# Zero-filled head tiles for the score products of two attentions, and other PSUM banks for half of the gating products

## The chip, the core and the metric

One Trainium2 chip; the kernel runs on one of its cores. The metric is device time in microseconds (us) of one execution, the median of several runs. TensorE (PE in the profile) does the matrix products, VectorE (DVE), ScalarE (ACT) and GpSimd (POOL) the rest, SyncE (SP) issues most transfers.

## The reference, cut to what matters

Two blocks over 512 tokens of 1024 features. The three places that the change touches:

```python
def chunk_band_attention(q, k, v, rel_bias):          # block 1, 8 heads of 64
    ...
    scores = jnp.einsum('bnqhd,bnkhd->bnhqk', qc, kb).astype(jnp.float32) * (d ** -0.5)
    ...
    scores = jnp.where(valid[None, :, None, None, :], scores + bias[None, None], NEG_INF)
    p = jax.nn.softmax(scores, axis=-1)
    out = jnp.einsum('bnhqk,bnkhd->bnqhd', p.astype(vb.dtype), vb)

# block 1, behind attention (y_a) and a linear recurrence (y_b)
merged = gate_a * (y_a @ proj_a[l]) + gate_b * (y_b @ proj_b[l])

def forgetting_attention(q, k, v, f_pre):             # block 2, layer 0, 8 heads of 64
    ...
    logits = jnp.einsum('bhqd,bhkd->bhqk', qb, k).astype(jnp.float32) * scale + fq[..., :, None] - F[..., None, :]
    logits = jnp.where(kpos[None, :] <= qpos[:, None], logits, -jnp.inf)
    p = jax.nn.softmax(logits, axis=-1)
```

## The kernel before, in words

**Dense products.** Activations lie with features on partitions and are split into a high and a low part; so are the weights, chunk by chunk: a DMA brings `raw`, ACT makes `whi` (L132), DVE makes `wlo` (L133). `dense_A` (L163) multiplies 256 output features at a time into two PSUM banks of [128, 512] with three products (high by high, low by high, high by low). The two banks come from a pool `mm` of two banks, unless the caller hands banks in (`ps=`). `dense_B` (L281) does the same with tokens on partitions.

**Attention** (`attention1` in block 1, the second half of `layer0` in block 2) runs in two halves of four heads. A half projects q, k and v for its heads. Two heads share a [128, 512] tile of q and one of k: the even head has rows 0 to 63, the odd one rows 64 to 127. Each of the two PSUM banks of a projection is evacuated in one ACT instruction over 128 rows (L1538 in block 1, L846 in block 2), with the factor 0.125, and in block 2 a bias, put on q.

`attention_heads` then goes over 16 units a half (4 heads by 4 query tiles of 128), software-pipelined: scores of unit u, transposes of unit u-1, values of unit u-2. A score (L1569) multiplies the 64 rows of its head, 128 queries against 128, 256, 384 or 512 keys; in f32 each is issued as two matmuls. In block 2 a bf16 matmul over 128 rows adds the causal mask (L1571). DVE adds the bias and finds the row minimum of the negated scores (L1573, `sb`, `sm`), ACT takes the exponential (L1575), PE transposes (L1583, `pspt`), ACT on even units (L1586) and DVE on odd ones (L1588) copy the transposes to `pT`, and PE forms the values (L1597, `pso`). Scores and transposes share one pool of PSUM banks.

**What fills PE meanwhile.** The order of all engines is set by a scheduler over the whole program, so matmuls of other phases stand between the units: in block 1 the recurrence of the other branch and dense products, in block 2 the mLSTM heads before, and dense products.

**mLSTM** (`mlstm`, block 2) stands before layer 0's attention. Its q tiles come from the ring with tag `q` of four buffers, one a head; `weigh` (L965, `pqk`) multiplies 128 rows of k and q. A head's end goes through POOL: a power on its statistics (L376, `st`) and four products with the output gate (L1004, `ho`), whose result PE transposes (L941, `psr`).

**Gating** (`gate_mul`, L598 to L600) is called for four pairs of feature tiles `fp` with `proj_a` behind the recurrence and four with `proj_b`: a `dense_A` into the two banks of `mm`, then DVE multiplies each bank with a gate (L600). The next call needs the same two banks. Two other pools of two banks, `ax` and `ax2`, serve the recurrence; `axt` (L1233) hands out their banks.

Of the kernel before, what the change touches and what calls it, by code (L numbers as in the profile page):

```python
# [26 lines left out]
# ---- per-feature vectors, features on partitions: name -> number of 128-columns  # L27
# [61 lines left out]
class Halves:  # L89
    """a tile [128, 2, 8, 256] (token half, feature tile, token) as [128 features, 512 tokens] of one feature tile"""  # L90
# [12 lines left out]
class Builder:  # L103
# [18 lines left out]
    # ---------------------------------------------------------------- weights  # L122
    def wchunk(self, src, a, b, keep=None):
        """a weight chunk of up to 1024 columns, split; keep: (pool, bufs) to hold it in"""
# [19 lines left out]
    def dense_A(self, xk, w, col0, pp, tag="mm", nf=2, half=None, ps=None, chunks=None, low=None):  # L144
        """nf feature tiles of W^T x, features on partitions; xk: [(hi, lo)] of [128, 512].
        half: only these 256 tokens (0 before 1, into the same banks); low: only the products with the weights'
        high (False, first) or low (True) parts"""
# [27 lines left out]
    def ahead(self, specs, pool):  # L175
        """the weights of begin, their low parts still to be made: (raw, hi, lo), the first two chunks
        in the ring of all weights; specs: (A or B, w, col0, columns)"""
# [18 lines left out]
    def ahead_hook(self, specs):  # L196
        """loads the next phase's first weights, when called"""
        def hook():
            self.nx_es.append(ExitStack())
            self.nx = self.ahead(specs, self.pool(self.nx_es[-1], "early", side="right"))  # L200
        return hook
# [22 lines left out]
    def begin(self, xk, specs):  # L224
        """the first products of a phase, the first half of the tokens before the last two tiles are there, from the
        weights loaded ahead; specs as there"""
# [32 lines left out]
    def dense_B(self, xk, w, col0, pp, tag="mm", width=512, toks=(0, 1, 2, 3), ps=None, chunks=None, low=None):  # L259
        """x W[:, col0:col0+width], tokens on partitions: {token tile: [128, width] PSUM view}; low: as in dense_A"""  # L260
# [26 lines left out]
    def close_B(self, xk, w, pp, add, post, T, pool, rest=None, lag=1, hook=None):  # L287
        """x W in two halves of the columns, the second token by token, so that what follows a token starts early;
        T: the transposes of a token, lag tokens late, the last ones in the next phase;
        rest: the tiles still to be added to the first half of the columns"""  # L290
# [16 lines left out]
    def mix_part(self, xk, w, pp):  # L307
        """column half 0: xN = ALPHA * xN + the part of the mixer's output that is ready"""
# [6 lines left out]
    def split(self, src, hi, lo, lo_eng=None):  # L315
        """hi + lo == src exactly; both of the tensor engine's reduced format"""
# [20 lines left out]
    def to_T(self, xn, n, pair, t, pp, tag, k0=0):  # L337
        """xn: [128 tokens, n*128] -> columns t of pair's tiles k0..k0+n, split"""
# [20 lines left out]
    # ------------------------------------------------------------ row vectors  # L359
# [12 lines left out]
    def rsqrt(self, out, src, n, scale, eps):  # L372
        """out = (scale * src + eps) ** -0.5 on [128, n] columns"""
# [21 lines left out]
    def ln_apply(self, x, st, g, b):  # L395
        """layer norm over 1024 features in place, eps 1e-5; st: bn_stats of the halves"""
# [19 lines left out]
    # ------------------------------------------------------------------ setup  # L416
# [48 lines left out]
    # ---------------------------------------------------------- block 1 mixer  # L465
    def block1_in(self, pool):
# [3 lines left out]
        with ExitStack() as es:  # L470
# [13 lines left out]
            # the tensor engine's clock rises only while it works  # L484
# [112 lines left out]
    def gate_mul(self, y, w, fp, gts):  # L597
        ps = self.dense_A(self.klist(y), self.A[w], fp * 256, self.mm)  # L598
        for f in range(2):
            self.nc.vector.tensor_tensor(gts[f], ps[f], gts[f], op=ALU.mult)  # L600
# [116 lines left out]
    # ------------------------------------------------- second block: shared  # L717
    def close_ln(self, xk, w, gn, bn, np_, pp, last=False, rest=None, hook=None):
        """xN = LN(xN + x w), then xT or the output; rest: xN's second half is still to be multiplied by ALPHA"""
# [73 lines left out]
    def log1pexp_neg_abs(self, out, u):  # L793
        """out = ln(1 + exp(-|u|))"""
# [885 lines left out]
```

## Time and profile before

| | |
|---|---|
| runs | 2109.14, 2109.42, 2111.05 us (median 2109.42) |
| span of the profiled execution, first to last instruction | 2106.5 us |
| own time of the profiled execution | not recorded; the shown runs lie 2.7 to 4.6 us above its span, their median 2.9 |
| PE busy | 2065.2 us, 98% |
| DVE, ACT, POOL busy | 1114.8, 765.6, 163.5 us |
| mean granted TensorE clock | 0.995 of full speed |

A row of the time line gives a start, a busy time, an engine, a line with its operation and names, and how many neighbouring instructions it joins; the bracket behind it is the engine's idle time before it and what ended that. Matmul ends are modelled, so a step on PE is read from start to start. One row can join the matmuls of several calls, and a score is two matmuls.

### The profile page before, as it was taken

The page shows a single profiled execution, that of the slowest core. Times are in us where ns is not written, and L with a number is a line of the kernel's source. Part 1 is how long each engine was busy: PE and PEld are TensorE (multiplying, and loading weights), DVE is VectorE, ACT ScalarE, POOL GpSimd, SP SyncE. Part 2 cuts the span into 40 slices and gives each one's busy share as a digit, 9 for nine tenths or more (in the row PEclk, how much of TensorE's full clock was granted, in tenths as well). Part 3 has the DMA queues.
Part 4 walks back from the last instruction along what each step waited for, and adds up shares of the span by engine and source line. Part 5 has one row for each costly group of instructions (what it writes and reads, how often), then busy time and mean ns, then how long its engine had stood idle before and what let it go on. Part 6 is the DMA issues. An engine that isn't in the chain of part 4 may idle for free.

```text
span 2106.5 us, 27707 instructions
## 1 busy us (share of the span) xinstructions
PE 2065.2 (98%) x11216; PEld 1696.1 (81%) x11216; DVE 1114.8 (53%) x1831; ACT 765.6 (36%) x1213; POOL 163.5 (8%) x258
## 2 busy tenths in 40 slices
PE   8999999999999999999999999999999999999998
PEld 6678677777888888888777888888897789888886
DVE  4554455565532424544534765435576676543565
ACT  4431552144333423333333344314334534432441
POOL 1101110110000000112200000000020310000000
PEclk9999999999999999999999999999999999999999
DMA  6241125143233334232212322333322033332332
GB/s 205 71 88 42 31 71 107 42 145 104 77 94 100 93 97 125 76 107 80 61 60 91 101 89 91 100 106 109 112 74 80 31 110 101 100 100 90 100 100 91
DMA packets 175120, 192.52 MB, mean 91 GB/s; under 512 B 31560, under 2 KB 144712, under 8 KB 174992
## 3 DMA queue, kind: packets, MB, share of 16 engines
q1 hardware_dynamic: 169920, 173.40, 27.4%
q0 software_dynamic: 5072, 17.35, 2.6%
q8 instruction: 88, 1.44, 0.3%
q14 instruction: 40, 0.33, 0.1%
HBM read 184.94 MB, written 5.78 MB: 91 GB/s over the span
## 4 chain that ended last, share of the span: by engine, by line
PE 53%; DVE 1%; DMA 1%; POOL 1%; ACT 0%; issue 0%; DVEq 0%; ACTq 0%; POOLq 0%
PE psA L163 29%; PE psB L281 19%; PE pss L1569 1%; PE pso L1597 1%; PE pho L1137 1%; DMA raw<-od_w_out 1%; PE psT L345 0%; PE pspt L1583 0%; PE ppg L1176 0%; PE pss L1571 0%; PE pqk L965 0%; PE pho L973 0%; DVE wlo L133 0%; PE psr L941 0%; ACT whi L132 0%
## 5 line engine op out<-in xcount | busy, mean ns | idle before, releaser
L133 DVE TENSOR_TENSOR wlo<-raw,whi 128x1024 fp32r<-128x1024 f32 (+1 forms) x295 | 360.3, 1224 | 506.9 <-ACT whi L132 303.3
L132 ACT ACTIVATE whi<-raw 128x1024 fp32r<-128x1024 f32 (+1 forms) x295 | 311.7, 1056 | 635.7 <-PE psA L163 288.4
L163 PE MATMUL psA<-xTh,whi 128*128 128x512 f32 (+1 forms) x1616 | 416.9, 378 | 3.6 <-ACT xTh L318 1.7
L163 PE MATMUL psA<-xTl,whi 128*128 128x512 f32 (+1 forms) x1616 | 415.8, 377 | 1.3 <-DVE st L375 1.3
L163 PE MATMUL psA<-xTh,wlo 128*128 128x512 f32 (+1 forms) x1616 | 412.1, 376 | 0.0
L163 PEld LDWEIGHTS psA<-xTh,whi 128*128 128x128 f32 x1616 | 288.8, 189 | 59.6 <-issue 3.0
L163 PEld LDWEIGHTS psA<-xTl,whi 128*128 128x128 f32 x1616 | 291.1, 190 | 56.2 <-issue 2.7
L163 PEld LDWEIGHTS psA<-xTh,wlo 128*128 128x128 f32 x1616 | 286.9, 188 | 53.3 <-issue 2.3
L772 DVE SCALAR_TENSOR_TENSOR v<-psA,par,v 128x511 f32<-128x511 f32 (+1 forms) x176 | 131.3, 747 | 78.9 <-ACT v L770 76.5
L376 POOL TENSOR_TENSOR st<-st,mhalf 128x1 f32<-128x1 f32 (+1 forms) x40 | 32.9, 822 | 1266.7 <-DVE st L375 1266.5
L281 PE MATMUL psB<-whi,hidh 128*128 128x512 f32 x480 | 126.7, 390 | 0.0
L281 PE MATMUL psB<-wlo,hidh 128*128 128x512 f32 x480 | 126.4, 389 | 0.0
L281 PE MATMUL psB<-whi,hidl 128*128 128x512 f32 x480 | 126.4, 389 | 0.0
L281 PEld LDWEIGHTS psB<-whi,hidl 128*128 128x128 f32 x480 | 90.1, 188 | 18.8
L281 PEld LDWEIGHTS psB<-wlo,hidh 128*128 128x128 f32 x480 | 90.1, 188 | 18.7
L281 PEld LDWEIGHTS psB<-whi,hidh 128*128 128x128 f32 x480 | 90.0, 188 | 18.7
L770 ACT ACTIVATE v<-psA,par 128x512 f32<-128x512 f32 x88 | 67.8, 771 | 98.0 <-PE psA L163 98.0
L281 PE MATMUL psB<-whi,xTh 128*128 128x256 f32 (+2 forms) x320 | 53.4, 289 | 0.0
L281 PE MATMUL psB<-whi,xTl 128*128 128x256 f32 (+2 forms) x320 | 52.6, 287 | 0.6 <-DVE xTl L319 0.6
L318 ACT ACTIVATE xTh<-psT 128x512 fp32r<-128x512 f32 x40 | 21.9, 595 | 84.2 <-PE psT L345 84.2
L281 PE MATMUL psB<-wlo,xTh 128*128 128x256 f32 (+2 forms) x320 | 49.3, 286 | 0.0
L1575 ACT ACTIVATE sb<-sb,sm 128x128 f32<-128x128 f32 (+1 forms) x64 | 35.7, 559 | 34.1 <-DVE sm L1573 33.5
(406 smaller groups left out, 2503.2 us busy)
## 6 DMA issues: line engine op xcount, KB each, us to landing
raw<-fup SPq DMA_DIRECT2D x88, 512.0 KB, 3.5
raw<-fdn SPq DMA_DIRECT2D x44, 512.0 KB, 3.3
raw<-w_in SPq DMA_DIRECT2D x42, 512.0 KB, 3.8
raw<-w_up SPq DMA_DIRECT2D x32, 512.0 KB, 3.8
raw<-w_down SPq DMA_DIRECT2D x32, 512.0 KB, 3.7
raw<-ev_w_in SPq DMA_DIRECT2D x26, 512.0 KB, 3.7
raw<-od_w_in SPq DMA_DIRECT2D x14, 512.0 KB, 3.8
raw<-w_out SPq DMA_DIRECT2D x8, 512.0 KB, 3.7
```

What stands on the lines that cost most here:

```text
L132: i = nc.scalar.activation(hi, raw, AF.Copy)
L133: self.w_ins = (i, nc.vector.tensor_tensor(lo, raw, hi.bitcast(F32), op=ALU.subtract))
L163: i = nc.tensor.matmul(o.rearrange("p (h t) -> p h t", h=2) if len(x.shape) == 3 else o, wt[:, k, fs], x, start=first and half != 1, stop= ...
L281: nc.tensor.matmul(ps[t], xk[k0 + k][a][:, t * 128 : t * 128 + 128], wt[:, k, :], start=first, stop=(end and k == kn - 1 and wt is lo), sk ...
L318: nc.scalar.activation(hi, src, AF.Copy)
L376: return nc.gpsimd.tensor_tensor(out, out, self.mhalf[:, 0:n], op=ALU.pow)
L770: nc.scalar.activation(v, ps[f], AF.Identity, scale=self.p(f"fcw{l}", 88 + ft), bias=self.p(f"fcb{l}", ft))
L772: nc.vector.scalar_tensor_tensor(v[:, sh:], ps[f][:, : 512 - sh], self.p(f"fcw{l}", tap * 44 + ft), v[:, sh:], op0=ALU.mult, op1=ALU.add)
L1137: nc.tensor.matmul(po[:, t, :], w[:, (t - j) * 128 : (t - j) * 128 + 128], xdt[j][:, h * 64 : h * 64 + 64], start=(j == 0 and t == 0), sto ...
L1569: nc.tensor.matmul(ps[:, 0:n], q[hs, t * 128 : t * 128 + 128], k[hs, 0:n], start=True, stop=cmask is None, skip_group_check=True)
L1575: nc.scalar.activation(sb[:, 0:n], sb[:, 0:n], AF.Exp, scale=-1.0, bias=sm[:, t : t + 1], accum_out=sm[:, 4 + t : 5 + t])
L1597: nc.tensor.matmul(po[:, t, :], pT[:, j * 128 : j * 128 + 128], v(j), start=(t == 0 and j == 0), stop=(j == t), skip_group_check=True)
```

## The change

Three edits.

1. `head_tiles`, new, makes four [128, 512] q tiles, one a head, and has POOL write zeros to the 64 rows that are the other head's. They are made once for both halves. A projection's bank is evacuated by two instructions: rows 0 to 63 by ACT into the even head's tile, rows 64 to 127 by DVE into the odd head's.
2. The score matmul takes all 128 rows of that q tile and of the k tile of two heads; the zero rows add nothing. k is as before. In layer 0 the four tiles come from the mLSTM's ring `q`, so a tile's zeros wait for the `pqk` products that read the buffer.
3. In `gate_mul`, calls with odd `fp` use two banks of `ax` and `ax2`.

```diff
     def gate_mul(self, y, w, fp, gts):
-        ps = self.dense_A(self.klist(y), self.A[w], fp * 256, self.mm)
+        ps = [self.axt(1, self.nm("psA")) for _ in range(2)] if fp % 2 else None
+        ps = self.dense_A(self.klist(y), self.A[w], fp * 256, self.mm, ps=ps)
...
     # layer0
+                fq = self.head_tiles(lp, 4, tag="q", bufs=4)
                 for hf in range(2):
-                    fq = featT(2056, "q", hf, 0.125, lambda f: bq[:, 4 + f : 5 + f])
+                    ps = self.dense_A(xk, W, 2056 + hf * 256, mm)
+                    for f in range(2):
+                        b = bq[:, 4 + 2 * hf + f : 5 + 2 * hf + f]
+                        nc.scalar.activation(fq[2 * f][0:64, :], ps[f][0:64, :], AF.Identity, scale=0.125, bias=b[0:64, :])
+                        nc.vector.tensor_scalar(fq[2 * f + 1][64:128, :], ps[f][64:128, :], 0.125, b[64:128, :], op0=ALU.mult, op1=ALU.add)
...
     # attention1
+        qz = self.head_tiles(ap, 4)
         for hf in range(2):
-            qk = []
-            for base, sc in ((0, 0.125), (512, 1.0)):
-                ps = self.dense_A(xk, w_in, base + hf * 256, mm)
-                row = []
-                for f in range(2):
-                    t = ap.tile([128, 512], F32, tag=f"qk{base}", bufs=2, name=self.nm("qk"))
-                    nc.scalar.activation(t, ps[f], AF.Copy, scale=sc)
...
+            ps = self.dense_A(xk, w_in, hf * 256, mm)
+            for f in range(2):
+                nc.scalar.activation(qz[2 * f][0:64, :], ps[f][0:64, :], AF.Copy, scale=0.125)
+                nc.vector.tensor_scalar(qz[2 * f + 1][64:128, :], ps[f][64:128, :], 0.125, None, op0=ALU.mult)
+            ps = self.dense_A(xk, w_in, 512 + hf * 256, mm)
...
+    def head_tiles(self, pool, n, **kw):
+        out = [pool.tile([128, 512], F32, name=self.nm("qz"), **kw) for _ in range(n)]
+        for h, t in enumerate(out):
+            self.nc.gpsimd.memset(t[64:128, :] if h % 2 == 0 else t[0:64, :], 0.0)
+        return out
...
     # attention_heads, scores
-            hs = slice((h % 2) * 64, (h % 2) * 64 + 64)
...
-            nc.tensor.matmul(ps[:, 0:n], q[hs, t * 128 : t * 128 + 128], k[hs, 0:n], start=True, stop=cmask is None, skip_group_check=True)
+            nc.tensor.matmul(ps[:, 0:n], q[:, t * 128 : t * 128 + 128], k[:, 0:n], start=True, stop=cmask is None, skip_group_check=True)
```

The order on PE stays as it was but for names, SP's does not change at all; POOL gains eight rows, DVE eight with two others joined. Two places follow. The changed kernel's line numbers are a few higher (L1004 becomes L1010, L957 L963, L1324 L1330, L1327 L1333).

POOL in the mLSTM, before, from the last mask of one head's weights to the statistics of the next (`w` is a tile of weights, `st` the statistics, `ho` a head's output):

```order
L957 AFFINE_SELECT w_1155_7926<-w_1155_7926 128x128
L376 TENSOR_TENSOR st_1150_7898<-st_1150_7898,mhalf_71 128x4
L957 AFFINE_SELECT w_1160_7943<-w_1160_7943 128x128
L1004 TENSOR_TENSOR ho_1140_7851<-ho_1140_7851,og_1094_7478 128x128
L1004 TENSOR_TENSOR ho_1140_7851<-ho_1140_7851,og_1095_7479 128x128
L1004 TENSOR_TENSOR ho_1140_7851<-ho_1140_7851,og_1096_7480 128x128
L1004 TENSOR_TENSOR ho_1140_7851<-ho_1140_7851,og_1097_7481 128x128
L957 AFFINE_SELECT w_1163_7960<-w_1163_7960 128x128
L957 AFFINE_SELECT w_1168_7997<-w_1168_7997 128x128
L957 AFFINE_SELECT w_1172_8011<-w_1172_8011 128x128
L376 TENSOR_TENSOR st_1167_7983<-st_1167_7983,mhalf_71 128x4
```

The same place of the changed kernel (`qz` is a zero-filled q tile):

```order
L963 AFFINE_SELECT w_1155_7934<-w_1155_7934 128x128
L1565 MEMSET qz_1184_8086 64x512
L376 TENSOR_TENSOR st_1150_7906<-st_1150_7906,mhalf_71 128x4
L963 AFFINE_SELECT w_1160_7951<-w_1160_7951 128x128
L1010 TENSOR_TENSOR ho_1140_7859<-ho_1140_7859,og_1094_7486 128x128
L1010 TENSOR_TENSOR ho_1140_7859<-ho_1140_7859,og_1095_7487 128x128
L1010 TENSOR_TENSOR ho_1140_7859<-ho_1140_7859,og_1096_7488 128x128
L1010 TENSOR_TENSOR ho_1140_7859<-ho_1140_7859,og_1097_7489 128x128
L963 AFFINE_SELECT w_1163_7968<-w_1163_7968 128x128
L963 AFFINE_SELECT w_1168_8005<-w_1168_8005 128x128
L1565 MEMSET qz_1185_8087 64x512
L376 TENSOR_TENSOR st_1167_7991<-st_1167_7991,mhalf_71 128x4
```

One memset now stands ahead of each of the two statistics; the mask of `w_1172` has gone behind the second.

DVE where block 1's first q projection ends, before (`ta`, `kkn`, `KB` belong to the recurrence's preparation, `wlo` to the weights):

```order
L1321 SCALAR_TENSOR_TENSOR KB_68_559<-kkn_70_561,eLm_63_547 128x4x128
L1323 TENSOR_SCALAR ta_65_553<-ta_65_553,d_kah_251 128x512
L1324 SCALAR_TENSOR_TENSOR ta_65_553<-ta_65_553,rkv_45_454 128x512
L133 TENSOR_TENSOR wlo_182_1340<-raw_180_1337,whi_181_1339 128x1024
L1327 SCALAR_TENSOR_TENSOR ta_65_553<-rkv_35_386,par_68,ta_65_553 128x512
L1331 TENSOR_TENSOR bon_72_574<-psb_71_572,rkv_55_522 128x512
```

And in the changed kernel:

```order
L1329 TENSOR_SCALAR ta_65_553<-ta_65_553,d_kah_251 128x512
L1542 TENSOR_SCALAR qz_166_1240<-psA_169_1247 64x512
L1330 SCALAR_TENSOR_TENSOR ta_65_553<-ta_65_553,rkv_45_454 128x512
L133 TENSOR_TENSOR wlo_184_1348<-raw_182_1345,whi_183_1347 128x1024
L1333 SCALAR_TENSOR_TENSOR ta_65_553<-rkv_35_386,par_68,ta_65_553 128x512
L1542 TENSOR_SCALAR qz_168_1242<-psA_170_1248 64x512
L1337 TENSOR_TENSOR bon_72_574<-psb_71_572,rkv_55_522 128x512
```

The first evacuation has gone in between two steps of `ta`, the second behind the last of them.

## Rows read from the trace of the kernel before

**Rows 1.** The page: busy time of each engine over the span, and the chain of work that ended last, by line.

```profile
PE 2065.2 (98%) x11216; PEld 1696.1 (81%) x11216; DVE 1114.8 (53%) x1831; ACT 765.6 (36%) x1213; POOL 163.5 (8%) x258
PE psA L163 29%; PE psB L281 19%; PE pss L1569 1%; PE pso L1597 1%; PE pho L1137 1%; DMA raw<-od_w_out 1%; PE psT L345 0%; PE pspt L1583 0%; PE ppg L1176 0%; PE pss L1571 0%; PE pqk L965 0%; PE pho L973 0%; DVE wlo L133 0%; PE psr L941 0%; ACT whi L132 0%
```

**Rows 2.** Busy time of each engine in two stretches, the first and the second half of block 1's attention: the stretch, its length, then busy time and instructions of PE, PEld, DVE, ACT and POOL, the granted clock, the share of the DMA engines and GB/s.

```profile
119.94:155.74 35.80, 35.80 (x189) 23.65 (x188) 22.85 (x80) 15.71 (x46) 3.68 (x9) 1.00 0.48 97
213.19:257.51 44.32, 42.42 (x244) 28.50 (x244) 22.35 (x63) 23.14 (x57) 6.37 (x11) 1.00 0.13 37
```

**Rows 3.** PE's time line in the first half of block 1's attention.

```profile
119.94 0.92 PE L1569 MATMUL pss<-qk,qk 64*128 64x128 f32 x4
...
124.29 0.40 PE L163 MATMUL psA<-xTh,wlo 128*128 128x512 f32 x1
124.62 1.12 PE L1569 MATMUL pss<-qk,qk 64*128 64x512 f32 x2
125.67 0.55 PE L1583 MATMUL pspt<-start,sb 128*128 128x128 f32 x3
126.05 0.56 PE L1597 MATMUL pso<-v,pT 128*128 128x64 f32 x4
```

**Rows 4.** PE's time line where dense products follow each other, and in the mLSTM, where f32 products over 128 rows (`pqk`) have other products over 128 rows on either side.

```profile
88.26 1.07 PE L163 MATMUL psA<-xTh,wlo 128*128 128x512 f32 x4
89.17 1.07 PE L163 MATMUL psA<-xTh,whi 128*128 128x512 f32 x4
...
993.61 1.02 PE L965 MATMUL pqk<-q,k 128*128 128x512 f32 x2
994.47 0.39 PE L973 MATMUL pho<-mv,w 128*128 128x129 f32 x2
...
998.42 0.39 PE L965 MATMUL pqk<-q,k 128*128 128x128 f32 x2
998.64 0.61 PE L973 MATMUL pho<-mv,w 128*128 128x129 f32 x4
```

**Rows 5.** PE's time line in layer 0's attention.

```profile
1051.51 0.50 PE L1583 MATMUL pspt<-start,sb 128*128 128x128 f32 x3
1051.94 0.48 PE L1569 MATMUL pss<-k,q 64*128 64x128 f32 x2
1052.35 0.23 PE L1571 MATMUL pss<-cm,idb 128*128 128x128 bf16 x1
...
1052.94 0.78 PE L1597 MATMUL pso<-fv,pT 128*128 128x64 f32 x6
```

**Rows 6.** The weight loads of TensorE (PEld) at the score of 124.62.

```profile
124.62 0.29 PEld L1569 LDWEIGHTS pss<-qk,qk 64*128 64x128 f32 x2 [0.36 <-DVE wk L1396]
```

**Rows 7.** Groups of PE instructions by line and shape, over the whole span: count, busy us and mean ns of one, idle time before.

```profile
L1569 PE MATMUL pss<-qk,qk 64*128 64x512 f32 x16 | 9.0, 641 | 0.0
...
L965 PE MATMUL pqk<-q,k 128*128 128x512 f32 x8 | 4.2, 606 | 0.0
```

**Rows 8.** Time line of DVE, PE and ACT at three places of the attentions: the first half of block 1, its second half, layer 0.

```profile
138.16 0.67 DVE L1588 COPY pT<-pspt 128x512 f32<-128x512 f32 x1
...
139.19 0.27 PE L1583 MATMUL pspt<-start,sb 128*128 128x128 f32 x1
...
240.13 1.28 ACT L1511 ACT_TABLE_LOAD   x1
...
243.28 0.44 PE L1583 MATMUL pspt<-start,sb 128*128 128x128 f32 x2 [1.90 <-ACT pT L1586]
...
1052.10 0.49 ACT L1586 ACTIVATE pT<-pspt 128x384 f32<-128x384 f32 x1 [1.14 <-PE pspt L1583]
```

**Rows 9.** Time line of PE and DVE in the gating: the first two calls with `proj_a` and the last two behind each other, and the product behind the last call with `proj_b`.

```profile
430.79 1.07 PE L163 MATMUL psA<-yah,wlo 128*128 128x512 f32 x4
433.38 1.21 PE L163 MATMUL psA<-yah,whi 128*128 128x512 f32 x4 [1.52 <-DVE gate L600]
...
442.24 1.17 PE L163 MATMUL psA<-yah,whi 128*128 128x512 f32 x4 [0.36 <-DVE gate L600]
...
481.69 2.14 PE L281 MATMUL psB<-whi,mgh 128*128 128x512 f32 x8 [0.78 <-DVE gate L600]
...
431.32 1.41 DVE L1516 SCALAR_TENSOR_TENSOR yT<-yT,par,bon 128x512 f32<-128x512 f32 x2
```

**Rows 10.** What an evacuation costs, and what stands by it: groups of DVE and ACT (a tensor by scalars from PSUM on DVE; the q and k tiles on ACT; the high part of a weight chunk on ACT, from the page), and PE's wait for `ta` in block 1.

```profile
L1275 DVE TENSOR_SCALAR sq<-pss 128x512 f32<-128x512 f32 x4 | 2.6, 680 | 0.0
...
L1538 ACT ACTIVATE qk<-psA 128x512 f32<-128x512 f32 x8 | 4.7, 592 | 13.5 <-PE psA L163 13.5
...
L132 ACT ACTIVATE whi<-raw 128x1024 fp32r<-128x1024 f32 (+1 forms) x295 | 311.7, 1056 | 635.7 <-PE psA L163 288.4
...
82.02 1.13 PE L1329 MATMUL psb<-ta,cst 128*128 128x512 f32 x2 [1.78 <-DVE ta L1327]
```

**Rows 11.** A memset of a whole tile on POOL (group), and the time line of POOL and PE in the mLSTM.

```profile
L818 POOL MEMSET gtok<- 128x512 f32 x1 | 0.6, 551 | 0.0
...
1006.23 1.02 POOL L376 TENSOR_TENSOR st<-st,mhalf 128x4 f32<-128x4 f32 x1 [0.19 <-PE pho L973]
...
1006.51 0.39 PE L965 MATMUL pqk<-q,k 128*128 128x128 f32 x2
...
1008.52 0.74 PE L941 MATMUL psr<-start,ho 128*128 128x128 f32 x2 [0.21 <-POOL ho L1004]
```

More of the change, by code (lines that the diff above doesn't have):

```diff
@@ L922, in layer0 @@
                     self.attention_heads(lb, [
-                        (fq[hh // 2], fk[hh // 2], hh, lambda j, hh=hh, fv=fv: fv[:, j, hh * 64 : hh * 64 + 64], os_[hh // 2],
+                        (fq[hh], fk[hh // 2], hh, lambda j, hh=hh, fv=fv: fv[:, j, hh * 64 : hh * 64 + 64], os_[hh // 2],
                          lambda hh=hh: fbias(4 * hf + hh), (idb, cm)) for hh in range(4)])
@@ L1529, in rbias @@
             return lambda t: b[:, 384 - 128 * t : 512]
+        qz = self.head_tiles(ap, 4)
         for hf in range(2):
-            qk = []
-            for base, sc in ((0, 0.125), (512, 1.0)):
-                ps = self.dense_A(xk, w_in, base + hf * 256, mm)
-                row = []
-                for f in range(2):
-                    t = ap.tile([128, 512], F32, tag=f"qk{base}", bufs=2, name=self.nm("qk"))
-                    nc.scalar.activation(t, ps[f], AF.Copy, scale=sc)
-                    row.append(t)
-                qk.append(row)
+            ps = self.dense_A(xk, w_in, hf * 256, mm)
[3 more added lines that the diff above has]
+            ps = self.dense_A(xk, w_in, 512 + hf * 256, mm)
+            kt = []
+            for f in range(2):
+                t = ap.tile([128, 512], F32, tag="k", bufs=2, name=self.nm("k"))
+                nc.scalar.activation(t, ps[f], AF.Copy)
+                kt.append(t)
             v = ap.tile([128, 4, 256], F32, tag="v", bufs=1, name=self.nm("v"))
@@ L1546, in attention1 @@
             self.attention_heads(ap, [
-                (qk[0][hh // 2], qk[1][hh // 2], hh, lambda j, hh=hh, v=v: v[:, j, hh * 64 : hh * 64 + 64], o[hh // 2],
+                (qz[hh], kt[hh // 2], hh, lambda j, hh=hh, v=v: v[:, j, hh * 64 : hh * 64 + 64], o[hh // 2],
                  lambda hh=hh: rbias(4 * hf + hh), None) for hh in range(4)])
```

## The prediction

> **What bounds the kernel now.** I read the page first, for the engine that sets the time: PE is busy for 98% of the span, and the chain that ended last runs through its dense products, with the score line L1569 and the values L1597 at 1% each [rows 1]. So only two things can shorten the kernel: less PE time where PE never rests, or one of its few waits taken out. Next I read the stretches of block 1's attention, for whether PE rests there: it does not in the first half (35.80 of 35.80 us) and for 1.90 us in the second (42.42 of 44.32) [rows 2]. DVE is busy for 22.85 us of the first stretch and ACT for 23.14 of the second, so both have room on average, which says little on single places. A PE that is busy is not a PE at its peak, so the third view is its time line from start to start, to see what a score costs beyond its columns. The last views are the waits at the gating, and what DVE and POOL do where the change puts new work.
>
> **The scores, gain.** A 64-row score stands between products over 128 rows, and its price shows in three steps.
> - Entry: the matmul ahead of the score at 124.62 takes 0.33 us from start to start (124.29 to 124.62) [rows 3]; in a row of dense products one takes 0.91 / 4 = 0.23 (88.26 to 89.17) [rows 4]. Difference 0.10. The score's weight load shows why: the load unit had been idle for 0.36 us and begins only at 124.62, with the matmul [rows 6], so a load onto 64 rows does not run under the 128-row matmul ahead.
> - The score itself: 128 queries by 512 keys take 1.05 (124.62 to 125.67) [rows 3]; the mLSTM's f32 product of the same 512 columns over 128 rows takes 0.86 (993.61 to 994.47) [rows 4]. Difference 0.19. By 128 keys it is 0.41 (1051.94 to 1052.35) [rows 5] against 0.22 (998.42 to 998.64) [rows 4]: 0.19 again, so it does not grow with the columns.
> - Exit: the three transposes behind the score take 0.38 (125.67 to 126.05) [rows 3]. Three ahead of a score take 0.43 (1051.51 to 1051.94) [rows 5], of which 0.10 is entry, so 0.33. Difference 0.05. In layer 0 the mask product follows at once, and I count no exit.
>
> Block 1 has 32 scores in 30 stretches (in two places two stand together, as the four matmuls at 119.94 [rows 3]): 30 x 0.34 = 10.2 us. Layer 0 has 32 singly: 32 x 0.29 = 9.3. Together **-19.5**. The means of single instructions would give far less, 641 against 606 ns [rows 7], 0.035 x 128 matmuls = 4.5 us. They hold the time from first to last column of one matmul, overlapped with the next; the steps are what PE pays, so I take these and keep 4.5 as the low end.
>
> Here a rule of the Trainium skill speaks against the change. In the trace loads over 128 rows do hide: a dense step is 0.23 us with nothing exposed [rows 4]. The Trainium skill ("TensorE: Matmul & The Clock Gate", Part 3, The mechanism) says that a weight load overlaps with matmuls in flight only when the row groups differ. By that rule the 128-row scores' loads would stay exposed as the 64-row ones are, and the whole sum below would be +0.4 us in place of -12.7. The trace disagrees with the rule for 128-row loads, and no better for the 64-row ones, which differ from what is in flight and wait all the same.
>
> **The scores, given back.** PE that is faster meets DVE and ACT earlier, and three places show little slack. In block 1 DVE's copy `pT` ends at 138.83 and PE needs it at 139.19: 0.36 spare [rows 8]. In its second half ACT, reloading tables (240.13), already holds PE for 1.90 at 243.28 [rows 8]; what scores ahead of that gain is lost there. In layer 0 ACT's `pT` ends at 1052.59 and PE's values start at 1052.94: 0.35 spare [rows 8, 5], where the head gains 4 x 0.29 = 1.16. The chain of a unit (score, DVE, ACT, transposes, copy, values) moves with its score, so most of a gain survives. I take 0.3 us a head lost in layer 0 and 0.5 in block 1, about a third: 8 x 0.3 + 8 x 0.5 = **+6.4**. That is chosen; its ends are 0 and three quarters, 14.6.
>
> **The gating.** The second call waits 1.52 us for DVE's product of the first, held up behind the recurrence's last steps (L1516 from 431.32) [rows 9]; from start to start 430.79 to 433.38 is 2.59 against 0.91 for such a group [rows 4], so 1.7 goes. The wait of 0.36 at 442.24 goes too. At 481.69 PE waits 0.78 before a product whose first banks were used by the last two gate products [rows 9]; only one of them now lies elsewhere, so I count half, 0.4. Sum **-2.5** (ends 0.4 and 3.0). Next late is nothing on PE: the banks of `ax` and `ax2` are free, the first `mm` banks have a whole call's time.
>
> **The evacuations.** A tile of q on ACT cost 0.59 [rows 10]. A half tile keeps its 512 columns, so I give it nearly the same on ACT, and 0.68 on DVE by the nearest row, a tensor by scalars from PSUM (L1275) [rows 10]. Eight DVE instructions are new, 5.4 us on an engine with 47% idle. In block 1's first half the first of them goes in ahead of L1324, and PE waits 1.78 for what follows on DVE and POOL (82.02) [rows 10]: one operation of 0.68 into a chain that PE waits for, **+0.7** (0 to 1.2, as it also has to wait for its bank). Behind each q projection stands k's in the same two banks. They come free after ACT's half and then DVE's, so 0.7 later. PE has other matmuls in between, and no row shows it waiting there; I take **+0.6** for the four places (0 to 2.8, four times the 0.7).
>
> **The zeros.** A memset over all rows takes 0.55 [rows 11]; half the rows, the same 512 columns, so I keep that. Block 1's four stand ahead of all of attention's work on POOL, which is busy for 8% of the span [rows 1], and need no data: nothing; without that cover they would cost 4 x 0.55 = 2.2 once. Two of layer 0's cost. The one ahead of `st_1150` waits for the `pqk` at 1006.51, whose two matmuls end at 1006.90; so `st` starts at 1006.90 + 0.55 = 1007.45 instead of 1006.23 [rows 11], 1.2 later. Behind it are DVE's normalization, `ho` on POOL and PE's transposes at 1008.52, which already wait for `ho` (0.21) [rows 11]: 1.2 of PE time. The other, ahead of `st_1167`, costs 0.55 less the mask that has gone behind, say 0.4. **+1.6** (0 to 2.2).
>
> **Sum.** -19.5 + 6.4 - 2.5 + 0.7 + 0.6 + 1.6 = -12.7 us. The profiled span is 2106.5 and would become 2093.8. That execution's own time is not recorded; the runs' median, 2109.4, stands 2.9 above the span, and I keep these 2.9: the forecast is 2109.4 - 12.7 = **2096.7**.
>
> **Rivals.**
> - *Nothing is given back.* For it: DVE is busy for 64% of the first stretch and ACT for 52% of the second [rows 2]. Against it: the 1.90 wait. -19.5 - 2.5 + 2.9 = -19.1, 2090.3; with the added costs at their low ends 2087.4. Chance 0.18.
> - *The chains of DVE and ACT become the bound.* For it: 0.35 spare at two places, and two attentions whose copies alternate between both engines. Attention then keeps a quarter: -4.9 - 2.5 + 2.9 = -4.5, 2104.9. Chance 0.13.
> - *No gain in the scores*, their weight loads being exposed over 128 rows too: 0 - 2.5 + 2.9 = +0.4, 2109.8. Against it the steps of 0.86 and 0.22 of `pqk` [rows 4]. Chance 0.03. It is the Trainium skill's rule named above.
> - *Slower: DVE's queue held by ACT.* Each new DVE half waits for ACT's half of the same bank, which may stand behind a weight chunk's high part (1.06) [rows 10]. Held behind it are `wlo` and the recurrence's steps, which PE needs. If every half costs PE all of 1.06 + 0.59 + 0.68 = 2.33 us, eight cost 18.6 in place of my 1.3: -12.7 - 1.3 + 18.6 = +4.6, 2114.0. It decides from 14.0 / 8 = 1.75 a place. Against it: `wlo` has under 1% of the chain that sets the time [rows 1]. Chance 0.03.
>
> **How the numbers follow.** The forecast has 0.63 and by its own bounds lies between about 2091 and 2102. The range goes down to 2088.0, into the first rival, and up to 2104.0; outside lie a fifth of that rival, most of the second, and the last two, together about 0.19. A measurement of this kernel tells 0.2%, 4.2 us, from no change, so faster means under 2105.2: 0.63 + 0.18 + 0.10 = 0.91; same 0.06; slower 0.03.
>
> **What would show it.** Score steps of 0.86 at 512 keys and 0.22 at 128 with no weight load starting after idle time: the gain. PE's waits for `pT` or `sb` in the attention stretches, near 6 us in sum: what is given back. No wait at the second gate call. PE's wait for `ho` ahead of the `psr` that now starts at 1008.52 some 1.2 longer. The prediction is wrong if score steps stay at 1.05, or if PE waits for copies by more than 10 us or not at all.

## The result, and the profile after

The changed kernel takes **2095.3 us** (median of 4 runs, 2093.56 to 2095.68) against 2110.24 for the kernel before on the same chip; ratio 0.9925, 95% interval [0.9913, 0.9937]. The forecast was 2096.7. Its profiled execution took 2095.37 us by its own time, span 2093.6.

PE is still the bound. The page of the changed kernel, busy times and the chain that ended last, by line:

```profile
PE 2052.4 (98%) x11216; PEld 1699.7 (81%) x11216; DVE 1120.4 (54%) x1839; ACT 766.0 (37%) x1213; POOL 165.0 (8%) x266
...
PE psA L163 28%; PE psB L281 18%; PE pss L1584 1%; PE pso L1612 1%; PE pho L1143 1%; PE psT L345 1%; PE pspt L1598 0%; PE ppg L1182 0%; PE pcb L1116 0%; DVE pa L1172 0%; DVE xbc L1082 0%; PE pc L1063 0%; ACT whi L132 0%; PE pxn L1099 0%; PE pss L1586 0%
```

PE has the same 11216 instructions [rows 1]. Unlike what the section on the change says, their order differs, but only in 29 places, at the end of block 1's first half and in the mLSTM, so the two traces can be laid side by side, instruction by instruction. The lengths between the same pairs of PE instructions give this table (us; my working from the two traces):

| stretch (time before) | before | after | gain | forecast |
|---|---|---|---|---|
| q evacuations, 70.1 to 82.0 | 11.88 | 12.61 | -0.73 | -0.7 |
| block 1 attention, first half | 35.80 | 31.39 | +4.41 | +6.2 for both halves |
| block 1 attention, second half | 44.32 | 42.25 | +2.07 | |
| gating, 430.8 to 485.1 | 54.28 | 51.30 | +2.98 | +2.5 |
| mLSTM, 984.1 to 1018.2 | 34.13 | 35.31 | -1.18 | -1.6 |
| behind layer 0's first q projection, 1018.2 to 1026.1 | 7.88 | 8.77 | -0.90 | -0.6 (four places) |
| layer 0 attention, first half | 31.24 | 26.87 | +4.38 | +6.9 for both halves |
| layer 0 attention, second half | 32.99 | 28.79 | +4.20 | |
| *sum of what the change touches* | | | *+15.23* | *+12.7* |
| 529.8 to 545.0, and `wlo` late behind it | | | +1.92 | none |
| 925 to 935, 1570 to 1585, 1630 to 1645 | | | -4.27 | none |
| all the rest, over 1700 us | | | -0.03 | none |
| first to last matmul | | | +12.85 | |

The two lines behind the sum are stages that the change does not touch. What differs there is mostly TensorE's clock. Rows of before and then of after (stretch, length, PE, PEld, DVE, ACT, POOL, granted clock, DMA share, GB/s):

```profile
529.75:545.04 15.29, 13.95 (x93) 13.72 (x94) 12.26 (x20) 3.99 (x9) 1.62 (x3) 0.78 0.24 74
925.08:935.05 9.97, 7.93 (x40) 6.31 (x39) 3.31 (x6) 4.10 (x6) 0.26 (x1) 1.00 0.49 154
```

```profile
521.17:533.84 12.67, 11.33 (x94) 11.09 (x95) 11.12 (x19) 3.99 (x9) 1.63 (x3) 1.00 0.19 62
914.62:926.14 11.52, 9.48 (x41) 7.43 (x40) 3.29 (x6) 4.10 (x6) 0.23 (x1) 0.85 0.45 134
```

Before, the granted clock was 0.78 in the first place and full in the second; after, it is full in the first and 0.85 in the second. The same 93 or 94 instructions take 2.62 us less in the first place, the same 40 or 41 take 1.55 us more in the second. In both kernels most such stretches, at 1.2 in place of 2.4 GHz, lie behind a wait of PE.

Now the steps, each read from the start of one instruction to the start of the next. PE's time line of the changed kernel at the places of [rows 3] and [rows 5]:

```profile
124.56 0.40 PE L163 MATMUL psA<-xTh,wlo 128*128 128x512 f32 x1
124.79 1.04 PE L1584 MATMUL pss<-k,qz 128*128 128x512 f32 x2
125.67 0.49 PE L1598 MATMUL pspt<-start,sb 128*128 128x128 f32 x3
126.00 0.56 PE L1612 MATMUL pso<-v,pT 128*128 128x64 f32 x4
...
1043.65 0.50 PE L1598 MATMUL pspt<-start,sb 128*128 128x128 f32 x3
1043.99 0.39 PE L1584 MATMUL pss<-k,qz 128*128 128x128 f32 x2
1044.21 0.22 PE L1586 MATMUL pss<-cm,idb 128*128 128x128 bf16 x1
```

The entry (the matmul ahead of the score) takes 0.23 us (was 0.33), the score of 512 keys 0.88 (1.05), the three transposes behind it 0.33 (0.38). In layer 0 three transposes ahead of a score take 0.34 (0.43) and the score of 128 keys 0.22 (0.41). Entry 0.10, the score itself 0.17 to 0.19, exit 0.05: the three prices of the forecast. They are paid once for a stretch of 64-row matmuls. Where two scores stand together (213.19 before), the steps from the matmul ahead on are 0.21, 0.21, 0.11, 0.22 and 0.31, and 0.12, 0.11, 0.11, 0.22 and 0.22 after the change: the two steps in between cost nothing. The weight loads of the same score [rows 6]:

```profile
124.71 0.30 PEld L1584 LDWEIGHTS pss<-k,qz 128*128 128x128 f32 x2 [0.18 <-DVE sm L1588]
```

The load now begins at 124.71, 0.08 before its matmul and under the one that started at 124.56. Before, the first load of 62 of the 64 scores began with its matmul; now that of 63 begins 0.05 to 0.42 ahead of it. Whether the late load makes the longer steps or only goes with them, no run separates; that the steps go with the rows, e4 shows below. One sentence of the Trainium skill ("TensorE: Matmul & The Clock Gate", Part 3, The mechanism) lets a load overlap matmuls in flight only where the row groups differ; another sentence of the same section also lets it run ahead into a background weight buffer. Both matmuls use all 128 rows here, and the load overlaps: the measurement decides against the first sentence for this case and agrees with the second.

What was given back shows in PE's idle time, the stretch's length less PE's busy time. The four halves of the attentions, columns as above:

```profile
120.68:152.07 31.39, 31.16 (x189) 24.05 (x188) 22.62 (x81) 16.13 (x46) 3.68 (x9) 1.00 0.54 91
209.47:251.72 42.25, 39.47 (x245) 29.55 (x244) 22.45 (x63) 23.27 (x58) 6.39 (x11) 0.96 0.14 38
1039.01:1065.88 26.87, 26.87 (x181) 21.18 (x179) 14.85 (x50) 14.09 (x42) 2.23 (x4) 1.00 0.18 51
1096.80:1125.59 28.79, 28.79 (x213) 24.20 (x212) 14.90 (x50) 14.02 (x42) 2.12 (x4) 1.00 0.20 65
```

PE rests for 0.23 us in block 1's first half, for 2.78 in its second, and not at all in layer 0. PE and ACT in block 1's second half:

```profile
237.60 0.44 PE L1598 MATMUL pspt<-start,sb 128*128 128x128 f32 x2 [2.78 <-ACT pT L1601]
```

```profile
227.75 1.28 ACT L1515 ACT_TABLE_LOAD   x1
...
230.65 1.28 ACT L1590 ACT_TABLE_LOAD   x1
...
232.45 1.28 ACT L1515 ACT_TABLE_LOAD   x1
...
234.45 1.28 ACT L1517 ACT_TABLE_LOAD   x1
...
237.29 0.25 ACT L1601 ACTIVATE pT<-pspt 128x128 f32<-128x128 f32 x1
```

From 226.91 to 237.54 ACT has almost no gap. Four table loads stand in it, 5.1 us, because the recurrence's group norm asks for logarithms (L1515) and their exponentials (L1517) between the softmax's exponentials (L1590). The same four stood there before the change. The wait of 1.90 [rows 8] has grown to 2.78, and behind it the clock falls (0.96 granted over the half, full before [rows 2]). Of the half's forecast 15 x 0.34 = 5.1 us, 2.07 arrived.

The gating [rows 9]:

```profile
424.96 1.07 PE L163 MATMUL psA<-yah,wlo 128*128 128x512 f32 x4
425.86 1.07 PE L163 MATMUL psA<-yah,whi 128*128 128x512 f32 x4
...
473.35 1.67 PE L281 MATMUL psB<-whi,mgh 128*128 128x512 f32 x6 [0.31 <-DVE gate L601]
```

There is no wait at the second call; of the last one's 0.78, 0.31 stays. The costs, PE at the first q projection, then POOL and PE in the mLSTM and behind layer 0's q projection [rows 10, 11]:

```profile
79.07 1.20 PE L163 MATMUL psA<-xTh,whi 128*128 128x512 f32 x4 [1.00 <-DVE qz L1542]
...
82.85 1.13 PE L1335 MATMUL psb<-ta,cst 128*128 128x512 f32 x2 [1.19 <-DVE ta L1333]
...
998.26 0.52 POOL L1565 MEMSET qz<- 64x512 f32 x1 [0.98 <-PE pqk L971]
998.87 1.02 POOL L376 TENSOR_TENSOR st<-st,mhalf 128x4 f32<-128x4 f32 x1
...
1001.22 0.74 PE L947 MATMUL psr<-start,ho 128*128 128x128 f32 x2 [1.22 <-POOL ho L1010]
...
1018.42 0.97 PE L163 MATMUL psA<-xTh,whi 128*128 128x512 f32 x3 [0.69 <-DVE qz L919]
```

### The profile page after: what moved, and what is told of

Read it like the earlier page. It is cut to its first block, busy times and chain, and to the rows that moved or that the text cites. A ratio compares the mean times of both kernels' runs of the same rounds, so it can differ in the third digit from the quotient of the medians.

```text
span 2093.6 us, 27722 instructions
## 1 busy us (share of the span) xinstructions
PE 2052.4 (98%) x11216; PEld 1699.7 (81%) x11216; DVE 1120.4 (54%) x1839; ACT 766.0 (37%) x1213; POOL 165.0 (8%) x266
## 4 chain that ended last, share of the span: by engine, by line
PE 50%; DVE 1%; ACT 0%; issue 0%; POOL 0%; DVEq 0%; ACTq 0%; POOLq 0%
PE psA L163 28%; PE psB L281 18%; PE pss L1584 1%; PE pso L1612 1%; PE pho L1143 1%; PE psT L345 1%; PE pspt L1598 0%; PE ppg L1182 0%; PE pcb L1116 0%; DVE pa L1172 0%; DVE xbc L1082 0%; PE pc L1063 0%; ACT whi L132 0%; PE pxn L1099 0%; PE pss L1586 0%
## 5 line engine op out<-in xcount | busy, mean ns | idle before, releaser
L1584 PE MATMUL pss<-k,qz 128*128 128x128 f32 (+3 forms) x128 | 46.2, 447 | 0.0
```

Source lines behind the costliest of these rows:

```text
L1584: nc.tensor.matmul(ps[:, 0:n], q[:, t * 128 : t * 128 + 128], k[:, 0:n], start=True, stop=cmask is None, skip_group_check=True)
```

## The experiments

Each kernel was laid against the kernel before in the same way. "Stretch" means the rows of the table above. Ratios are to the kernel before on the same chip.

**One part at a time.** e1: only `gate_mul` changed. e2: only `attention1`, with `hs` kept for layer 0. e3: only `layer0`, with `hs` kept for block 1.

```diff
# e2: scores, q tiles of layer 0 as before
+            hs = slice(0, 128) if cmask is None else slice((h % 2) * 64, (h % 2) * 64 + 64)
# e3: the same with "cmask is not None", q tiles of block 1 as before
```

> Only the gating's banks are changed; scores and tiles as before. Theory (the three parts add up, each with its own place on PE's time line): PE's waits at the second and fourth gate call go and the one ahead of the product behind gating is cut, together -3.0 us, as the same stretch measured with all three parts (430.8 to 485.1: 54.3 us before, 51.3 after). Rival (the gating's gain is taken back where the next stage starts, the weights' split being late): under -1 us. Stretches at the lower clock may move either by 2 us.

> Only block 1's attention has zero-filled tiles and 128-row scores; layer 0 and gating as before. Theory: the first q projection costs 0.7 (PE 70.1 to 82.0), the first half of the attention gives 4.4, the second 2.1 after what ACT's table loads and the clock take back: -5.8 us. Rival (the two attentions and the gating help each other, a part alone gives less): under -3. Rival (nothing taken back when the other parts are missing): -9.5.

> Only layer 0's attention has zero-filled tiles and 128-row scores; block 1 as before. Theory: the two halves give 4.4 and 4.2, the zeros in POOL's queue cost 1.2 in the mLSTM, the late bank behind the q projection 0.9: -6.5 us. Rival (most of a gain in block 1 moves clock and waits later on, so that layer 0 alone gives another sum): outside -4.5 to -8.5.

| | ratio, interval | stretches touched (gain) | largest other differences in the profile |
|---|---|---|---|
| e1 | 0.9994 [0.9985, 1.0003] | gating 2.99 | 82 to 120: -1.82, lower clock |
| e2 | 0.9974 [0.9963, 0.9985] | -0.73, 4.37, 2.12 | 529.8 to 545: +2.63, 925: -1.63, 1570: -1.59, 1630: -1.25 |
| e3 | 0.9977 [0.9968, 0.9987] | -1.17, -0.90, 4.35, 4.21 | 82 to 120: -1.81, 529.8: +1.26, 925: -1.63, 1570: -1.60, 1630: -1.38 |

Each stretch gives alone what it gives with the others, within 0.1 us: the parts add up, 3.0 + 5.8 + 6.5 = 15.3. The medians do not, 1.2 + 4.9 + 4.3 = 10.4 us; e3's 4.3 lies just outside the 4.5 to 8.5 that were expected, while its stretches give 6.5. In the profiles most of what lies between is stretches at the lower clock, at the same few places every time; that the medians lack the same is not shown run by run. e1 alone is not told from no change by its runs; its gain stands on the trace.

**The rows alone.** e4 keeps tiles, evacuations, zeros and gating and takes the rows back.

```diff
+            hs = slice((h % 2) * 64, (h % 2) * 64 + 64)
-            nc.tensor.matmul(ps[:, 0:n], q[:, t * 128 : t * 128 + 128], k[:, 0:n], ...
+            nc.tensor.matmul(ps[:, 0:n], q[hs, t * 128 : t * 128 + 128], k[hs, 0:n], ...
```

> Everything of the change but the rows: zero-filled tiles, evacuations by two engines and gating stay, and each score multiplies only the 64 rows of its head, as before. Theory (the gain is in the 128 rows alone, the rest of the two attention edits only costs): score steps of 1.05 us at 512 keys again, the two halves of each attention as long as before, and gating -3.0 + evacuations and zeros 0.7 + 1.2 + 0.9 = about 0 against the kernel before, 13 to 15 above the changed kernel. Rival (the gain comes from ACT's shorter evacuations and another order): half of the gain or more stays, -7 or below.

Measured 2111.14, ratio 1.0001 [0.9991, 1.001]. PE's time line at the same score, and the four attention stretches (columns as above):

```profile
126.63 1.12 PE L1585 MATMUL pss<-k,qz 64*128 64x512 f32 x2
127.68 0.55 PE L1599 MATMUL pspt<-start,sb 128*128 128x128 f32 x3
```

```profile
121.95:157.71 35.76, 35.76 (x189) 23.84 (x188) 22.87 (x81) 15.68 (x46) 3.68 (x9) 1.00 0.49 96
215.15:259.49 44.34, 42.43 (x244) 28.49 (x244) 22.36 (x63) 23.16 (x57) 6.37 (x11) 1.00 0.12 36
1047.01:1078.25 31.24, 31.24 (x179) 21.12 (x179) 15.12 (x50) 14.14 (x42) 2.24 (x4) 1.00 0.16 44
1109.20:1142.18 32.98, 32.98 (x214) 23.82 (x212) 15.08 (x50) 14.27 (x42) 2.12 (x4) 1.00 0.17 57
```

The step is 1.05 again and the stretches are as long as before the change; the costs (-0.73, -1.18, -0.90) and the gating's 2.98 stay. The whole gain in attention is the rows. The rival, that shorter evacuations and another order make the gain, falls.

**The rows without their costs.** e5 multiplies the pair's q tile as it was before, without zeros. It leaves out the separation of the heads: each score holds the sum over two.

```diff
-                (qz[hh], kt[hh // 2], hh, ...
+                (qk[0][hh // 2], qk[1][hh // 2], hh, ...
# scores over 128 rows as in the change; layer 0 likewise
```

> The changed kernel without zero-filled tiles: q is evacuated as before, by ACT in one instruction a bank, and a score multiplies all 128 rows of the q tile of two heads, so that it holds the sum over both heads (the separation of the heads is left out). Gating as in the change. Theory (the score's gain comes with the rows, the tiles and evacuations only cost, at three places): the attention stretches as short as in the changed kernel (31.4, 42.3, 26.9 and 28.8 us), and 0.7 at 70 to 82 us, 1.2 in the mLSTM, 0.9 behind the q projection saved: PE's ledger 2.8 us ahead of the changed kernel, but for stretches at the lower clock. Rival (zero rows are part of the gain, or the DVE halves also slow the attention): attention stretches over 0.5 us off.

Measured 2091.92, ratio 0.9912 [0.9898, 0.9927]. The attention stretches are 31.47, 42.22, 26.86 and 28.79 us, the three others 11.87, 34.12 and 7.88, as before the change. So zeros and evacuations cost 2.8 us at just these three places and nothing inside the attentions.

**What is given back.** e6 pairs the logarithms.

```diff
-            nc.tensor.matmul(pv, self.c("bones", 128), gsq[f], start=True, stop=True)
+            self.pv_mm = nc.tensor.matmul(pv, self.c("bones", 128), gsq[f], start=True, stop=True)
-        lns = [...]
+        lns = [...]; self.order(self.pv_mm, lns[0])
```

> The changed kernel with one more edge in the order: the logarithm of the first half of the recurrence's group norm waits for the matmul of the second, so both logarithms stand together on ACT and two of four table loads go from its chain at 227 to 237 us. Theory (what block 1's second half gives back is ACT's table loads: PE waits 2.78 us for pT at 237.6, and the clock falls behind that wait): the wait under 0.5, no stretch at the lower clock at 239, the second half 213 to 257 (42.3 us in the changed kernel) at 38 us. Rival (another chain, DVE's or the scores' banks, ends just as late): over 41 us.

Measured 2093.05, ratio 0.9912 [0.9897, 0.9927]. ACT, PE and the stretch:

```profile
231.81 1.28 ACT L1515 ACT_TABLE_LOAD   x1
233.11 1.26 ACT L1515 ACTIVATE gsq<-psv,d_c 128x512 f32<-128x512 f32 x2
234.39 1.28 ACT L1517 ACT_TABLE_LOAD   x1
```

```profile
237.38 0.44 PE L1598 MATMUL pspt<-start,sb 128*128 128x128 f32 x2 [0.41 <-ACT sb L1590]
```

```profile
211.04:248.94 37.90, 37.49 (x246) 28.39 (x244) 22.45 (x63) 20.84 (x56) 6.43 (x11) 1.00 0.14 43
```

Two loads are gone, the wait is 0.41, the clock stays full, the half takes 37.9 us in place of 42.2. Of those 4.3 us, 2.4 are the wait; the rest goes with the clock. The two profiled spans differ by only 2.2, since the clock fell elsewhere: 82 to 120 is 1.4 longer and 529.8 to 545 takes 15.23 again, while 925 to 935 is back at 9.99.

**The zeros.** e7 orders all four of layer 0's memsets behind the mLSTM's last output product, e9 each behind the one of the head before.

```diff
# e7
+            i = self.nc.gpsimd.memset(...); kw and self.order(self.last_ho, i)
# e9
+            i = self.nc.gpsimd.memset(...); kw and h and self.order(self.ho_i[h - 1], i)
```

> The changed kernel with layer 0's four memsets ordered behind the last of the mLSTM's output products on POOL. Theory (the 1.2 us lost in the mLSTM is two memsets that stand ahead of a head's statistics): 984 to 1018 takes 34.1 us again, as before the change, instead of 35.3, and the first score does not wait. Rival (the time is lost to the evacuations' DVE work in that stretch): 35 us or more. Rival (the memsets now delay the attention's first bias or score): the gain comes back as a wait ahead of the first score.

> The changed kernel with each of layer 0's memsets, but the first, ordered behind the output products of the mLSTM head before it on POOL, where POOL is idle, in place of behind the last head's. Theory (two memsets ahead of a head's statistics cost the 1.2 us, and the loss behind them came from the evacuations that the earlier edit moved back): 984 to 1018 takes 34.4 us or less instead of 35.3, 1018 to 1026 stays at 8.8. Rival (any delay of the zeros comes back at the q projection): 1018 to 1026 at 10 or more.

e7: 2097.77, ratio 0.9937 [0.9922, 0.9952]. The mLSTM takes 34.38 us where the theory has 34.1, but from there to the first score (1018 to 1046) PE needs 32.76 us, 28.55 in the changed kernel:

```profile
1014.24 1.16 PE L947 MATMUL psr<-start,ho 128*128 128x128 f32 x3 [1.27 <-POOL ho L1010]
1016.46 0.47 PE L947 MATMUL psr<-start,ho 128*128 128x128 f32 x1 [1.06 <-POOL ho L1010]
1017.03 2.04 PE L163 MATMUL psA<-xTh,whi 128*128 128x512 f32 x4
```

The scheduler has moved the last head's transposes, which stood behind the k projection, ahead of it. There PE waits for POOL's `ho` twice, and the four matmuls behind that take 1.84 us from start to start (0.91 at full clock). The rival that the gain comes back as a wait was right, though the wait is not at the first score. e9: 2091.74, ratio 0.9909 [0.9894, 0.9924]; the mLSTM takes 34.41 us, 1018 to 1026 stays at 8.87 and 1018 to 1046 takes 28.65. So 0.9 of the 1.18 goes when the memsets stand elsewhere in POOL's queue. The other 0.25 us is not shown to be theirs: e2, which has no zeros in layer 0, takes 34.38 there too, where e5, also without them, takes 34.12. Where the difference comes from stays open.

**The evacuations.** e8 deals them out by bank.

```diff
+                for e in range(2):
+                    rs = slice(64 * e, 64 * e + 64)
+                    if f == 0:
+                        nc.scalar.activation(qz[2 * f + e][rs, :], ps[f][rs, :], AF.Copy, scale=0.125)
+                    else:
+                        nc.vector.tensor_scalar(qz[2 * f + e][rs, :], ps[f][rs, :], 0.125, None, op0=ALU.mult)
```

> The changed kernel with the four half evacuations of a q projection dealt out by bank: ACT takes both halves of the first bank, DVE both of the second. Theory (what is lost behind the q projections is the first bank's wait for DVE, whose queue holds other work): PE's wait of 1.00 at 79.07 and of 0.70 at 1018.4 go, 0.7 + 0.9 saved. Rival (the second bank, now two instructions of DVE, is as late): less than 0.5 saved in sum; rival (DVE's two halves in a row hold what PE needs next): more is lost than before.

Measured 2093.58, ratio 0.9917 [0.99, 0.9933]. PE's waits at the same places:

```profile
81.96 1.13 PE L1339 MATMUL psb<-ta,cst 128*128 128x512 f32 x2 [1.61 <-DVE ta L1337]
95.27 1.10 PE L1339 MATMUL psb<-ta,cst 128*128 128x512 f32 x2 [1.29 <-DVE ta L1337]
...
1017.39 0.93 PE L163 MATMUL psA<-xTh,whi 128*128 128x512 f32 x3 [0.56 <-DVE qz L923]
```

The wait of 1.00 in block 1 is gone, and the second wait for `ta` is 1.29, where it is 2.20 in the changed kernel; 70 to 120 takes 49.1 us, against 50.4 in the changed kernel and 49.8 before it. In layer 0 the wait only falls from 0.69 to 0.56. PE waits there for the second bank, which DVE still evacuates, behind the mLSTM's norm. Half of the theory holds.

By their runs alone e5, e6, e7, e8 and e9 are not told from the changed kernel, since the intervals overlap; what each gains or loses stands on the stretches.

**All together.** e10 joins e6, e9 and, in block 1, e8; in layer 0 ACT makes all four halves. e11 is the same with layer 0's evacuations as in the change. e12 is the changed kernel again, on the same chip.

> The changed kernel with all that the runs found: the paired logarithms, the memsets behind each head's output products, block 1's evacuations dealt out by bank, and in layer 0 all four half evacuations on ACT, since DVE is held there by the mLSTM's norm. Theory (the parts lie at separate places of PE's time line and add): 4.4 in block 1's second half, 1.4 at 70 to 120, 0.9 in the mLSTM, 0.9 behind layer 0's q projection: 7 to 8 us under the changed kernel, 2087 to 2089, the stretches at the lower clock moving that by 2 either way. Rival (they displace each other or the clock takes it): less than 3 us under the changed kernel.

> As the run before, but with layer 0's evacuations as in the changed kernel (ACT the even half, DVE the odd half). Theory: PE's wait of 0.7 for DVE's half at the k projection of layer 0 stays, 0.7 to 0.9 us slower than the run before, all in 1018 to 1026. Rival (ACT with four halves holds the second bank for as long): the same or faster.

> The changed kernel itself, beside the two combined ones on the same chip. Theory: 2095 us, the stretches as measured before: 31.4, 42.3, 26.9 and 28.8 us in the attentions, 51.3 in the gating. If the stretches at the lower clock are what differs between executions, all other stretches repeat within 0.1 us.

| | median us (range) | ratio, interval |
|---|---|---|
| e10 | 2089.4 (2087.41 to 2092.16) | 0.9899 [0.9884, 0.9914] |
| e11 | 2087.6 (2084.17 to 2092.59) | 0.9884 [0.9866, 0.9901] |
| e12, the changed kernel | 2093.78 (2092.96 to 2096.0) | 0.9921 [0.9909, 0.9933] |

The stretches of e10: block 1's second half, the mLSTM, the place behind layer 0's q projection:

```profile
208.24:246.15 37.91, 37.49 (x245) 28.39 (x244) 22.46 (x63) 20.84 (x56) 6.41 (x11) 1.00 0.15 43
971.26:1005.42 34.16, 31.29 (x171) 22.92 (x170) 27.49 (x109) 15.18 (x42) 18.93 (x38) 1.00 0.11 34
1005.42:1013.28 7.86, 7.78 (x37) 6.35 (x36) 5.58 (x21) 4.67 (x7) 4.29 (x7) 1.00 0.01 3
```

42.2, 35.3 and 8.8 in the changed kernel; 70 to 120 takes 49.1 in place of 50.4. Every part is there and they add to 7.7 us; e11's last stretch is 8.86, so ACT's four halves are worth 1.0. The medians lie 4.4 and 6.2 us under e12's, and e11, 1.0 longer by its stretches, has the lower one. The clock goes with that: e11's runs with a mean granted clock of 0.996 took 2084.17 and 2086.23, the one with 0.992 took 2092.59. e11's interval lies below e12's, so this version beats the changed kernel by its runs; e10's overlaps e12's. Which of the two is better the runs don't tell. e12 repeats the first trace in every stretch that the change touches (31.41, 42.20, 26.87, 28.78, gating 51.30), save 70 to 120, where the clock falls and 1.5 us are added.

## Why the prediction was right

The forecast, 12.7 us under the median of the runs shown then, came out as 14.9 between medians on one chip, and 12.9 between the profiled spans. The mechanism of the main term is shown. That the sum fits this closely is in part luck: the stretches touched gained 15.2, and the clock, which had no term, took 2.35 back. The steps, one by one:

- **Scores, -19.5.** The mechanism was right: steps of 0.88 and 0.22 where 0.86 and 0.22 were forecast, and e4 shows that nothing else makes the gain. The size was somewhat high. PE does not rest in layer 0's attention in either kernel, so the 8.58 gained there is the price itself, 0.27 a score where the forecast had 0.29. In block 1's first half the 4.41 gained and a new wait of 0.23 make 0.31 a stretch where it had 0.34. In the second half 2.07, the 0.88 that the wait grew and some 1.7 of clock make 0.31 again; the 1.7 is an estimate, 0.04 of 42.25 us. Together that is about 17.9. Starts, not mean durations, were the thing to read: the means fell only from 641 to 614 ns.
- **Given back, +6.4.** By the same count about 2.8: the attentions together gained 15.06. In layer 0, where 2.4 was taken, nothing was given back; no copy held PE there. In block 1, where 4.0 was taken, it was not even by heads: 0.2 in the first half and 2.6 in the second, at the one wait for ACT and in the clock behind it, as e6 shows. PE's waits in these stretches are 3.0 us and not the 6 that the prediction looked for, and 1.9 of them were there before. So the two terms of the scores were both too large, by 1.6 and 3.6, against each other.
- **Gating, -2.5.** 2.98, in e1 and in all kernels that carry it.
- **Evacuations, +0.7 and +0.6.** 0.73 and 0.90. The second is one place of four, layer 0's first half. In block 1's first half PE also waits 1.00 for its bank, and then less for `ta` (1.19 for 1.78): the two costs overlap, so the sum is not both. In the two second halves PE has enough in between. A bank does not come free 0.7 after ACT's half, as was reckoned: DVE's half begins 1.95 us after ACT's has ended in block 1 (76.37 to 78.32) and 1.83 in layer 0 (1015.78 to 1017.61), behind DVE's other work.
- **Zeros, +1.6.** 1.18, of which 0.9 goes with the memsets' place (e9). PE's wait for `ho` ahead of the first transposes is 1.22; it was 0.21 before, and in e9 it is 0.47. So the memset ahead of the first statistics cost 0.75 to 1.0 there, where 1.2 was forecast, and the other one less than the 0.4 that was taken.
- **The clock** stood in no term. In the profiled pair it took 2.35 us net outside the stretches touched, and by other executions it can take or give some 3. The range had no reason in it for that.
- **From span to time, 2.9.** The runs of the changed kernel lie 1.7 to 1.8 us over their spans. By that the traced execution of the kernel before took about 2108.2 us, an estimate, less than any run shown then. So about 1 of the 2.9 was the difference between one execution and the median. The later median, 2110.24, is 2 above that execution, and so the medians give 14.9 where the spans give 12.9.

Of the rivals, the one without anything given back held in layer 0, and the one in which ACT becomes the bound is true for one place of block 1. DVE's queue held by ACT cost 1.6 us in all, far from the 14.0 at which it decides.

## What to carry to other kernels

An f32 product over 64 of 128 rows (two matmuls of PE) between products over all rows costs about 0.3 us beyond its columns here, at 128 keys as at 512. Zero rows that fill it up gained 15.1 us in the attentions and cost 2.8 at three places. The price is one per stretch of 64-row products, so putting such products side by side might save part of it too; no run tried that. Lay two traces side by side by PE's instruction order before explaining a difference of medians: the stretch that changed names itself to 0.1 us, when the medians scatter by 3. Put new work on a side engine behind what others wait for, not ahead of it, and look at what the scheduler moves when you order it.

## What the runs showed that was not expected

- The lower of TensorE's two clocks was granted at the same few places in most kernels of this study (near 85 to 97, 240, 530, 920, 1565, 1620 and 1648 us), all but the one near 1565 behind a wait of PE of 1.2 to 2.8 us; but which of them it was differed between kernels and between executions of one. A place costs 1.0 to 1.8 us (2.6 at 530 in the kernel before, once 4.0, at 1642 in e11). Runs of one kernel go with it: e11's differ by 8 us over a mean granted clock of 0.996 to 0.992. Why a place has it in one execution and not in the next was not settled.
- Taking a wait away can take away more than its length: in e6 a wait shorter by 2.4 us made the stretch 4.3 shorter, with the clock at 1.00 instead of 0.96.
